# The first feed-forward's gate and up products by the seven-product scheme, in two phases

## The chip, the cores and the metric

The kernel runs on one core of one Trainium2 chip. The metric is the device time of one execution in microseconds (us). Three runs of the kernel before gave 2999.54, 3005.77 and 3012.02 us; the median is 3005.77 us.

## The reference

Two transformer blocks over 1024 tokens of width 1024, in fp32. The change touches the feed-forward of the first block, a gated unit with 2816 = 22 x 128 hidden channels and a convolution over three neighbouring tokens on the gate:

```python
x = x + conv_glu(rmsnorm(x, norm_ffn_g[i]), w_ffn_gate[i], w_ffn_up[i],
                 ffn_conv_w[i], ffn_conv_b[i], w_ffn_down[i])

def conv_glu(h, w_gate, w_up, conv_w, conv_b, w_down):
    S = h.shape[1]
    a = h @ w_gate
    u = h @ w_up
    pad = CONV_WIDTH // 2
    ap = jnp.pad(a, ((0, 0), (pad, pad), (0, 0)))
    c = conv_b
    for j in range(CONV_WIDTH):
        c = c + ap[:, j:j + S] * conv_w[j]
    return (jax.nn.gelu(c, approximate=False) * u) @ w_down
```

The second block's feed-forward, which shares code with it after the change, is `f = square(relu(rms_norm(h) @ w_ff1)); h = h + f @ w_ff2` with 4096 = 32 x 128 hidden channels.

## The kernel before

All activations lie transposed, channels on the 128 partitions and the 1024 tokens along the free axis, so a tile is 128 x 1024. Each fp32 product is made of three matmuls on rounded parts: a weight is split into WH (rounded on ScalarE) and WL (the rest, on GpSimd or VectorE), an activation into H and L, and a product is WH.H + WL.H + WH.L. A matmul has a 128 x 128 weight and 512 token columns. The engines run in the order in which their instructions are written; in the first block's mixing part and the second's two strings of digits set how chains are merged, and elsewhere the code's own order holds.

The first feed-forward is `dense_ffn1` (L1383). For each of the 22 channel tiles m, `gate_up(m)` runs two strips of 48 matmuls (`strip`, L253): 8 input tiles x 3 matmuls x 2 token halves. The gate strip leaves through VectorE (`a`, L1393, times the norm factor R), then the convolution is three VectorE instructions (L1397 to L1399), the gelu is ScalarE's (L531), and GpSimd multiplies by R (L1401). The up strip leaves through a VectorE product with that (L1405), and the result f[m] is split into parts (L699, L700). f stays in SBUF: after each group of FF_PARTS tiles come the down products of that group, added to the residual x (L1326), which stays in SBUF too. Weights come through a ring of four slots (`w_use`), one 512 KB load and one split each (L207, L209).

The second feed-forward already runs in two phases. In `ff1` (L1968) the up products go by the Winograd form of Strassen's algorithm. A unit is two neighbouring channel tiles; the 8 input tiles are 4 pairs. With the activations' blocks x11, x12, x21, x22 and their sums T1 to T4 (`wino_tile`, L610 to L660, made by VectorE in L628, split in L621 and L626) a unit takes seven products of 12 matmuls each (P1 to P7) where the plain form takes eight. Units 0 and 1 come first with P1 and P2 ("lead"), then units 2 and 3 run in the plain form (C11 to C22) while T1 to T4 are being made, then the rest: P6, P5, P7 of a unit, P1 and P2 of the next but one, P4 and P3. The weights' sums S (L428) are GpSimd's, the splits ScalarE's (L452) and VectorE's or, for P1 and P2, GpSimd's (L454); they are prepared up to seven products ahead. Intermediate results are copied out of PSUM by ScalarE (L2005, L2010, L2014) and added by VectorE (L2007, L2016, L2027); relu and the factor R are VectorE's (L2018, L2019, L2028), the square ScalarE's (L2032). P5 and P3 of a unit share one PSUM bank, and two banks (`psd`) serve P5/P3 and P2 in turn. f and the residual go to DRAM (`scr_f`, on SP's queue), and in the second phase, `dense_ff2`, they come back (`fl`, `xr`), f is split again, and the down products run.

## Time and profile before

| | us |
|---|---|
| median of three runs | 3005.77 |
| profiled execution | 3010.28 |
| its span, first to last instruction | 3008.5 |
| TensorE busy (PE) | 2853.0 |
| VectorE busy (DVE) | 1599.3 |
| ScalarE busy (ACT) | 1059.6 |
| GpSimd busy (POOL) | 992.8 |

The profile shows one execution. The 1.8 us between the execution's time and its span lie around the first and the last instruction. Matmuls overlap, so a busy TensorE is judged by the distance from the start of one matmul to the start of the next, not by its busy time. The mean granted clock over the span is 0.98 of full speed.

### The profile page before, as it was taken

How to read it: one execution, taken by the hardware profiler on the slowest of the kernel's cores; microseconds unless marked ns; L12 is line 12 of the kernel's file. 1: busy time of each engine (PE TensorE's matmuls, PEld its weight loads, DVE VectorE, ACT ScalarE, POOL GpSimd, SP SyncE). 2: the span in 40 equal slices, each digit the busy share in tenths (PEclk: the TensorE clock that was granted, in tenths of full speed). 3: DMA queues.
4: the chain of work that ended last, by engine and by line, in shares of the span. 5: the costliest groups of instructions: out<-in, count | busy, mean ns of one | idle time of the engine just before them, and what ended most of it. 6: DMA issues, size and time to landing. Idle time of an engine off the chain costs nothing. (4 is left out here: it accounts for less than half of the span.)

```text
span 3008.5 us, 34910 instructions
## 1 busy us (share of the span) xinstructions
PE 2853.0 (95%) x14216; PEld 2364.8 (79%) x14216; DVE 1599.3 (53%) x1847; ACT 1059.6 (35%) x1480; POOL 992.8 (33%) x630
## 2 busy tenths in 40 slices
PE   8999999989899999999999999878899999999999
PEld 7878878877688888887878787656677778888877
DVE  7377676897732323324336376667685444333343
ACT  4345444554411111111234435454454334211141
POOL 2321115574322322222344244343313432322141
PEclk9999999989999999999999999989899999999999
DMA  3322124231111111111112221133132325422112
GB/s 127 81 53 65 59 74 158 76 120 36 35 42 51 62 36 63 35 50 42 56 56 92 70 71 44 42 112 98 36 112 105 110 108 211 160 78 90 36 56 84
DMA packets 65025, 232.71 MB, mean 77 GB/s; under 512 B 7776, under 2 KB 8544, under 8 KB 64864
## 3 DMA queue, kind: packets, MB, share of 16 engines
q1 hardware_dynamic: 33952, 119.31, 11.0%
q10 hardware_dynamic: 27072, 98.58, 10.3%
q0 software_dynamic: 3840, 12.59, 2.0%
q8 instruction: 112, 1.84, 0.3%
q14 instruction: 49, 0.40, 0.0%
HBM read 170.68 MB, written 46.14 MB: 72 GB/s over the span
## 5 line engine op out<-in xcount | busy, mean ns | idle before, releaser
L209 POOL TENSOR_TENSOR WL<-raw,WH 128x1024 fp32r<-128x1024 f32 x160 | 403.1, 2520 | 918.9 <-ACT WH L207 850.2
L1326 DVE TENSOR_TENSOR xr<-xr,psd 128x512 f32<-128x512 f32 x296 | 202.2, 685 | 389.2 <-PE psd L253 386.7
L253 PE MATMUL ps_f<-xL,WH 128*128 128x512 f32 x832 | 324.7, 390 | 6.3 <-DVE xL L588 6.3
L253 PE MATMUL ps_f<-xH,WH 128*128 128x512 f32 x832 | 325.4, 391 | 3.7 <-DVE xr L1326 3.7
L253 PE MATMUL ps_f<-xH,WL 128*128 128x512 f32 x832 | 323.9, 389 | 0.0
L207 ACT ACTIVATE WH<-raw 128x1024 fp32r<-128x1024 f32 x188 | 197.7, 1053 | 337.0 <-PE psd L253 246.9
L253 PE MATMUL psd<-xH,WH 128*128 128x512 f32 x568 | 233.0, 410 | 2.7 <-DVE cv L1659 1.6
L253 PE MATMUL psd<-xL,WH 128*128 128x512 f32 x568 | 223.6, 394 | 0.0
L253 PE MATMUL psd<-xH,WL 128*128 128x512 f32 x568 | 223.4, 393 | 0.0
L253 PEld LDWEIGHTS ps_f<-xL,WH 128*128 128x128 f32 x832 | 156.5, 188 | 39.7 <-DVE xL L588 7.2
L253 PEld LDWEIGHTS ps_f<-xH,WH 128*128 128x128 f32 x832 | 156.5, 188 | 37.7 <-ACT sq L601 4.1
L253 PEld LDWEIGHTS ps_f<-xH,WL 128*128 128x128 f32 x832 | 156.5, 188 | 33.0 <-issue 0.8
L1401 POOL TENSOR_TENSOR ge<-ge,R 128x1024 f32<-128x1024 f32 x22 | 52.7, 2397 | 387.6 <-ACT ge L531 387.6
L531 ACT ACTIVATE ge<-ge 128x1024 f32<-128x1024 f32 x22 | 23.4, 1062 | 375.7 <-DVE ge L1399 375.7
L280 PE MATMUL psd<-WH,xH 128*128 128x256 f32 x448 | 129.9, 290 | 11.5 <-DVE hgst L977 8.8
L1943 DVE TENSOR_TENSOR_SCAN rem<-rem,ones 128x1024 f32<-128x1024 f32 (+7 forms) x64 | 91.4, 1429 | 81.7 <-POOL rem L1941 81.7
L253 PEld LDWEIGHTS psd<-xH,WH 128*128 128x128 f32 x568 | 108.1, 190 | 26.2 <-issue 4.8
L280 PE MATMUL psd<-WL,xH 128*128 128x256 f32 x448 | 128.0, 286 | 0.7 <-POOL WL L209 0.7
L280 PE MATMUL psd<-WH,xL 128*128 128x256 f32 x448 | 127.8, 285 | 0.0
L253 PEld LDWEIGHTS psd<-xL,WH 128*128 128x128 f32 x568 | 107.7, 190 | 23.7
L253 PEld LDWEIGHTS psd<-xH,WL 128*128 128x128 f32 x568 | 108.0, 190 | 21.7 <-issue 1.7
L469 PE MATMUL psd<-x,WH 128*128 128x512 f32 x352 | 116.6, 398 | 6.8 <-ACT fr L2024 4.6
(853 smaller groups left out, 7095.9 us busy)
## 6 DMA issues: line engine op xcount, KB each, us to landing
raw<-w_in ACTq DMA_DIRECT2D x54, 512.0 KB
scr_f<-fr SPq DMA_DIRECT2D x32, 512.0 KB
fl<-scr_f SPq DMA_DIRECT2D x32, 512.0 KB
raw<-w_ff ACTq DMA_DIRECT2D x32, 512.0 KB
raw<-w_gate ACTq DMA_DIRECT2D x22, 512.0 KB
raw<-w_up ACTq DMA_DIRECT2D x22, 512.0 KB
raw<-w_down ACTq DMA_DIRECT2D x22, 512.0 KB
raw_a<-w_ff SPq DMA_DIRECT2D x18, 512.0 KB
```

The costliest lines, as they stand in the source:

```text
L207: nc.scalar.activation(out=self.WH[:, s], in_=raw, func=AF.Copy)
L209: eng.tensor_tensor(out=self.WL[:, s], in0=raw, in1=self.WH[:, s].bitcast(F32), op=ALU.subtract)
L253: nc.tensor.matmul(ps, a, b[:, hs], start=(i == 0), stop=(i == n - 1))
L280: nc.tensor.matmul(ps, a[:, ts], b, start=(i == 0), stop=(i == 23))
L469: self.nc.tensor.matmul(ps, x[:, js], y, start=(fresh and j == 0 and e == 0), stop=(j == 3 and e == 2), skip_group_check=True)
L531: self.nc.scalar.activation(func=func, **kw)
L1326: self.nc.vector.tensor_tensor(out=self.x[m][:, hs], in0=self.x[m][:, hs], in1=ps, op=ALU.add)
L1401: nc.gpsimd.tensor_tensor(out=ge, in0=ge, in1=self.R, op=ALU.mult)
L1943: nc.vector.tensor_tensor_scan(out=rem[:, 0:w], data0=rem[:, 0:w], data1=self.one_col.to_broadcast([P, w]), initial=1.0, op0=ALU.mult, op1 ...
```

## The change

The first feed-forward gets the second's form. Gate and up strips become units (11 pairs of channel tiles, gate and up in turn, 22 units), and their products go by the seven-product scheme, units 2 and 3 again in the plain form. The residual goes to DRAM on entry (`wino_entry`), f goes to DRAM as it is made, and the down products follow in a phase of their own (`dense_down`, now shared) with the groups (2, 4, 4, 4, 4, 4). The shared code of the up phase is `wino_up`. After a gate tile is done, its convolution, its gelu and its product with R are put on a list, and one of them is issued after each product of 12 matmuls (`todo`); where an up tile needs a factor that is not made yet, the list is run up to it. The product with R moves from GpSimd to VectorE, and so do the WL splits of P1 and P2 in this phase, but for the two lead units. Changed for both feed-forwards: the plain units take C11 and C12 of both units before C21 and C22; the activations' blocks are made in another rhythm (`steps`); and at the start of the phase the weights are prepared at least three products ahead, where it was four. The list of weights in the ring is 44 entries shorter.

```diff
-FF_PARTS = (4, 4, 4, 4, 2, 4)
+FF_PARTS = (2, 4, 4, 4, 4, 4)
...
+    add("w_down", *range(NFF))
...
+def wino_order(n, lead, plain):
+
+    order = [(u, k) for u in range(lead) for k in ("P1", "P2")]
+    order += [(u, k) for ks in (("C11", "C12"), ("C21", "C22")) for u in range(lead, lead + plain) for k in ks]
+    head = len(order)
+    rest = [u for u in range(n) if not lead <= u < lead + plain]
+    order += [(u, "P6") for u in range(2)]
+    for u in rest:
+        order += [(u, k) for k in ("P6", "P5", "P7")[u < 2:]]
+        later = [v for v in rest if v > u and v >= lead]
+        if later and u >= lead - 1:
+            order += [(later[0], "P1"), (later[0], "P2")]
+        order += [(u, "P4"), (u, "P3")]
+    return order, head
...
-        eng = nc.gpsimd if k in ("P1", "P2") else nc.vector
+        eng = nc.gpsimd if k in ("P1", "P2") and (self.wq["n"] < 2 * self.wq["lead"] or self.wq["units"][0][0] == "w_ff1") else nc.vector
...
-            self.wino_ready(i + min(7, max(4, (i - q["head"]) // 2)))
+            self.wino_ready(i + min(7, max(3, (i - q["head"]) // 2)))
...
+    def wino_entry(self, st, m, gname):
+
+        self.wino_tile(st, m, self.x[m], gname, self.scr_f[NFF2 + m])
+        self.x[m] = None
+        if m in (3, 5, 6, 7):
+            self.wino_square(st)
+        if m in (1, 2, 3, 4, 6, 7):
+            self.wino_ready((1, 2, 3, 4, 6, 7).index(m))
...
+                if j == 2 and b == 0:
+                    units = [(mat, 2 * p) for p in range(NFF // 2) for mat in ("w_gate", "w_up")]
+                    self.wino_begin(units, 2, 2)
+                    self.wino_load(3)
...
-                        self.norm_tile(self.st, m, self.x[m], "ffn_g")
+                        self.wino_entry(nst, m, "ffn_g")
...
-            self.merge(self.dense_ffn1(al))
+            self.up1(al)
+            self.merge(self.dense_down("w_down", FF_PARTS, "ple_g"))
...
+    def up1(self, al):
+
+        nc = self.nc
+        g = {}
+
+        todo = self.todo = []
+
+        def factor(u, t):
+            if u % 2 == 0:
+                return self.R
+            while (u - 1, t) not in g:
+                todo.pop(0)()
+            return g[u - 1, t]
+
+        def done(u, t, a):
+            m = u // 2 * 2 + t
+            if u % 2:
+                g.pop((u - 1, t))
+                nc.sync.dma_start(out=self.scr_f[m], in_=a)
+                return
+
+            v = {}
+
+            def conv():
+                ge = v["ge"] = self.U("ge")
+                w = lambda j: self.col("conv_w", j * NFF + m)
+                nc.vector.tensor_scalar(out=ge, in0=a, scalar1=w(1), scalar2=self.col("conv_b", m), op0=ALU.mult, op1=ALU.add)
+                nc.vector.scalar_tensor_tensor(out=ge[:, 0:S - 1], in0=a[:, 1:S], scalar=w(0), in1=ge[:, 0:S - 1], op0=ALU.mult, op1=ALU.add)
+                nc.vector.scalar_tensor_tensor(out=ge[:, 1:S], in0=a[:, 0:S - 1], scalar=w(2), in1=ge[:, 1:S], op0=ALU.mult, op1=ALU.add)
+
+            def gelu():
+                self.act(AF.Gelu, out=v["ge"], in_=v["ge"])
+
+            def times_r():
+                ge = g[u, t] = v.pop("ge")
+                nc.vector.tensor_tensor(out=ge, in0=ge, in1=self.R, op=ALU.mult)
+
+            todo.extend((conv, gelu, times_r))
+
+        self.wino_up(al, factor, lambda out, x, y: nc.vector.tensor_tensor(out=out, in0=x, in1=y, op=ALU.mult), done)
 
...
+    def up2(self, al):
+
+        nc = self.nc
+        self.todo = []
+
+        def done(u, t, y):
+            nc.scalar.activation(out=y, in_=y, func=AF.Square)
+            nc.sync.dma_start(out=self.scr_f[2 * u + t], in_=y)
+
+        self.wino_up(al, lambda u, t: self.R, lambda out, x, y: nc.vector.scalar_tensor_tensor(out=out, in0=x, scalar=0.0, in1=y, op0=ALU.max, op1=ALU.mult), done)
+
+    def wino_up(self, al, factor, mul, done):
+
+        nc = self.nc
+        st, self.st = self.st, None
         norm = self.norm_steps(st)
         plain = []
-
         head = self.wq["head"]
-        steps = lambda i: 3 if i < 2 else 2 if i < 4 or i in (6, 9) or i > head - 3 else 1
+        steps = lambda i: 3 if i < 2 else 2 if i < 4 else 1 if i < 8 else 0 if i < head - 2 else 3 if i < head else 2
 
...
+            if self.todo:
+                self.todo.pop(0)()
             if i > 7 and plain:
-                m, y = plain.pop(0)
-                nc.vector.scalar_tensor_tensor(out=y, in0=y, scalar=0.0, in1=self.R, op0=ALU.max, op1=ALU.mult)
-                done(m, y)
+                u, t, y = plain.pop(0)
+                mul(y, y, factor(u, t))
+                done(u, t, y)
...
             elif k == "P4":
-                nc.vector.scalar_tensor_tensor(out=e["y1"][:, lo], in0=ps, scalar=0.0, in1=R(lo), op0=ALU.max, op1=ALU.mult)
-                nc.vector.scalar_tensor_tensor(out=e["y1"][:, hi], in0=e["y1"][:, hi], scalar=0.0, in1=R(hi), op0=ALU.max, op1=ALU.mult)
-                done(2 * u + 1, e.pop("y1"))
+                y = e.pop("y1")
+                mul(y[:, lo], ps, factor(u, 1)[:, lo])
+                mul(y[:, hi], y[:, hi], factor(u, 1)[:, hi])
+                done(u, 1, y)
...
             else:
-                nc.vector.tensor_tensor(out=e["y0"][:, hi], in0=ps, in1=e.pop("u")[:, lo], op=ALU.add)
-                nc.vector.scalar_tensor_tensor(out=e["y0"], in0=e["y0"], scalar=0.0, in1=self.R, op0=ALU.max, op1=ALU.mult)
-                done(2 * u, e.pop("y0"))
-
-        def done(m, y):
-            nc.scalar.activation(out=y, in_=y, func=AF.Square)
-            nc.sync.dma_start(out=self.scr_f[m], in_=y)
+                y = e.pop("y0")
+                nc.vector.tensor_tensor(out=y[:, hi], in0=ps, in1=e.pop("u")[:, lo], op=ALU.add)
+                mul(y, y, factor(u, 0))
+                done(u, 0, y)
...
             if left == 8:
-                self.halt = len(self.seq)
+                self.halt = self.halts.pop(0)
...
+    def dense_down(self, mat, parts, gname):
+
+        f = self.f
...
+        k0 = blk = 0
+        for j, n in enumerate(parts):
+            last = j == len(parts) - 1
+            ks = range(k0, k0 + n)
+            k0 += n
+            ahead = [] if last else [list(range(k0, k0 + parts[j + 1]))[b * parts[j + 1] // n:(b + 1) * parts[j + 1] // n] for b in range(n)]
+            for b in range(n):
+                s = self.w_use(mat, blk)
+                blk += 1
+                for k in ahead[b] if ahead else []:
+                    if k == len(self.fl):
+                        self.ff_load(k)
+                for i in range(8 // n):
+                    m = 8 // n * b + i
...
+                        self.norm_tile(nst, m, self.x[m], gname)
+                if b and ahead:
+                    for k in ahead[b - 1]:
+                        if k not in f:
+                            self.ff_part(k)
+            for k in ahead[-1] if ahead else []:
+                if k not in f:
+                    self.ff_part(k)
...
-    a["w_up"] = _strips(g["w_ffn_up"][0])
+    a["w_gate"] = _strips(g["w_ffn_gate"][0], True)
+    a["w_up"] = _strips(g["w_ffn_up"][0], True)
```

On VectorE, in the first feed-forward, one channel tile before (`a` is the gate's result, `ge` the factor, `f1L` the low part of f):

```order
L1393 TENSOR_TENSOR a<-ps_f,R 128x512 x2
L1397 TENSOR_SCALAR ge<-a,cols 128x1024
L1398 SCALAR_TENSOR_TENSOR ge<-a,cols,ge 128x1023
L1399 SCALAR_TENSOR_TENSOR ge<-a,cols,ge 128x1023
L1405 TENSOR_TENSOR ge<-ps_f,ge 128x512 x2
L700 TENSOR_TENSOR f1L<-ge,f1H 128x1024
```

And now, from P4 of a gate unit (its `fr<-ps_f,R`) to the convolution of its other tile:

```order
L1430 TENSOR_TENSOR fr<-ps_f,R 128x512
L1430 TENSOR_TENSOR fr<-fr,R 128x512
L1417 TENSOR_SCALAR ge<-fr,cols 128x1024
L1418 SCALAR_TENSOR_TENSOR ge<-fr,cols,ge 128x1023
L1419 SCALAR_TENSOR_TENSOR ge<-fr,cols,ge 128x1023
L443 TENSOR_TENSOR WL<-raw_b,WH 128x512
L2026 TENSOR_TENSOR fr<-psd,u_6776 128x512
L1430 TENSOR_TENSOR fr<-fr,R 128x1024
L443 TENSOR_TENSOR WL<-S_6785,WH 128x512
L1426 TENSOR_TENSOR ge<-ge,R 128x1024
L443 TENSOR_TENSOR WL<-S_6879,WH 128x512
L1417 TENSOR_SCALAR ge<-fr,cols 128x1024
```

The convolution of one tile (L1417 to L1419) now stands ahead of the add that empties the bank of P3 (`fr<-psd,u`, L2026), and the product with R (L1426) stands on VectorE behind a gelu of ScalarE.

On ScalarE, in the second feed-forward before, from one unit's P1 copy (`fr<-ps_f`) to the next unit's P6 copy (`u<-ps_f`):

```order
L2005 COPY fr<-ps_f 128x512
L452 ACTIVATE WH<-raw_a 128x512 x2
L2032 ACTIVATE fr<-fr 128x1024
L452 ACTIVATE WH<-raw_b 128x512
L2032 ACTIVATE fr<-fr 128x1024
L452 ACTIVATE WH<-S_16022 128x512
L2010 COPY u_16152<-ps_f 128x512
```

And in the first feed-forward now, from the same copy of a gate unit to the P6 and P7 copies of the up unit behind it:

```order
L2002 COPY fr<-ps_f 128x512
L441 ACTIVATE WH<-raw_a 128x512 x2
L441 ACTIVATE WH<-raw_b 128x512
L520 ACTIVATE ge<-ge 128x1024
L441 ACTIVATE WH<-S_6785 128x512
L2007 COPY u_6916<-ps_f 128x512
L441 ACTIVATE WH<-S_6879 128x512 x2
L2011 COPY u_6916<-ps_f 128x512
L520 ACTIVATE ge<-ge 128x1024
```

The two squares (L2032) have no counterpart here; a gelu (L520) stands ahead of the P6 copy (L2007), and one behind the P7 copy (L2011).

## Rows read from the trace of the kernel before

**Rows 1.** The page's shares by engine: busy us (share of span) xinstructions.
```profile
PE 2853.0 (95%) x14216; PEld 2364.8 (79%) x14216; DVE 1599.3 (53%) x1847; ACT 1059.6 (35%) x1480; POOL 992.8 (33%) x630
```

**Rows 2.** Three stretches: length; PE, PEld, DVE, ACT, POOL busy; clock; DMA share, GB/s.
```profile
788.10:1524.20 736.10, 725.67 (x3174) 597.73 (x3174) 262.20 (x299) 135.22 (x135) 214.75 (x89) 0.99 0.15 49
...
2285.20:2526.00 240.80, 237.45 (x1034) 193.22 (x1035) 113.83 (x141) 92.38 (x149) 99.06 (x72) 1.00 0.33 121
2537.60:2896.00 358.40, 355.71 (x1560) 291.94 (x1558) 135.07 (x165) 82.18 (x81) 106.64 (x43) 1.00 0.30 103
```

**Rows 3.** TensorE's timeline, first feed-forward: start, duration, line, idle before.
```profile
787.91 0.39 PE L253 MATMUL psd<-oh3L,WH 128*128 128x512 f32 x1
792.00 0.47 PE L253 MATMUL ps_f<-xH,WH 128*128 128x512 f32 x1 [3.71 <-DVE xr L1326]
...
801.49 0.80 PE L253 MATMUL ps_f<-xL,WH 128*128 128x512 f32 x1 [3.99 <-DVE xL L588]
...
1524.17 0.39 PE L253 MATMUL ps_t<-xH,WH 128*128 128x512 f32 x1
```

**Rows 4.** TensorE's timeline, second feed-forward: two product starts in the steady part.
```profile
2512.12 0.39 PE L469 MATMUL ps_f<-x,WH 128*128 128x512 f32 x1
...
2514.84 0.39 PE L469 MATMUL psd<-x,WH 128*128 128x512 f32 x1
```

**Rows 5.** TensorE's matmuls of the second feed-forward's up phase, L469 alone, by count.
```profile
2200.00:2545.00 345.00, 319.10 (x1368) 257.42 (x1368) 0.99 0.32 115
```

**Rows 6.** TensorE's timeline, second feed-forward's up phase: begin, stalls of the start, end.
```profile
2203.47 0.39 PE L469 MATMUL ps_f<-x,WH 128*128 128x512 f32 x1
...
2261.04 0.59 PE L469 MATMUL psd<-x,WH 128*128 128x512 f32 x1 [2.95 <-ACT fr L2024]
...
2285.41 0.49 PE L469 MATMUL ps_f<-xT,WH 128*128 128x512 f32 x1 [0.68 <-ACT u L2014]
...
2537.57 0.39 PE L253 MATMUL psd<-f0H,WH 128*128 128x512 f32 x1
```

**Rows 7.** All engines, end of a unit of the second feed-forward: start, duration.
```profile
2501.45 0.85 DVE L2019 SCALAR_TENSOR_TENSOR fr<-fr,R 128x512 f32<-128x512 f32 x1
...
2503.41 1.30 POOL L428 TENSOR_TENSOR S<-raw_a,S 128x512 f32<-128x512 f32 x1
...
2503.95 1.31 DVE L454 TENSOR_TENSOR WL<-raw_b,WH 128x512 fp32r<-128x512 f32 x1 [1.65 <-ACT WH L452]
2505.19 0.68 DVE L2027 TENSOR_TENSOR fr<-psd,u 128x512 f32<-128x512 f32 x1
...
2507.16 1.06 ACT L2032 ACTIVATE fr<-fr 128x1024 f32<-128x1024 f32 x1 [3.24 <-DVE fr L2028]
...
2508.65 0.56 ACT L2010 COPY u<-ps_f 128x512 f32<-128x512 f32 x1
```

**Rows 8.** TensorE behind that copy.
```profile
2509.26 0.50 PE L469 MATMUL ps_f<-xT,WH 128*128 128x512 f32 x1 [0.30 <-ACT u L2010]
```

**Rows 9.** The gelu chain of the first feed-forward: count, min/median/max ns.
```profile
L1397 DVE TENSOR_SCALAR ge<-a,cols x22: 811/812/814, 813.0 to 1469.7; 128x1024 f32<-128x1024 f32 x22
L1398 DVE SCALAR_TENSOR_TENSOR ge<-a,cols,ge x22: 1283/1284/1287, 813.8 to 1470.5; 128x1023 f32<-128x1023 f32 x22
...
L531 ACT ACTIVATE ge<-ge x22: 1060/1062/1062, 816.4 to 1473.2; 128x1024 f32<-128x1024 f32 x22
```

**Rows 10.** Line L454, all its splits on VectorE of one kind.
```profile
L454 DVE TENSOR_TENSOR WL<-S,WH x56: 679/692/1776, 2258.2 to 2518.4; 128x512 fp32r<-128x512 f32 x56
```

**Rows 11.** Groups in 2295 to 2525 us: count, busy us, mean ns, idle before.
```profile
L428 POOL TENSOR_TENSOR S<-raw_b 128x512 f32<-128x512 f32 x12 | 16.4, 1365 | 0.0
...
L2028 DVE SCALAR_TENSOR_TENSOR fr<-fr,R 128x1024 f32<-128x1024 f32 x12 | 15.5, 1289 | 0.4
...
L2018 DVE SCALAR_TENSOR_TENSOR fr<-ps_f,R 128x512 f32<-128x512 f32 x12 | 8.3, 692 | 21.3 <-PE ps_f L469 21.3
```

**Rows 12.** DMA rate in 2510 to 2600 us, 40 slices of 2.25 us.
```profile
GB/s 297 381 421 401 195 7 233 169 300 229 0 0 0 269 377 364 410 421 419 411 404 417 404 410 410 381 42 0 0 0 0 253 235 302 149 206 27 233 13 220
```

More of the change, by code (lines that the diff above doesn't have):

```diff
@@ L81, in weight_order @@
     add("w_out", *range(8))
-    k = 0
-    parts = []
-    for n in FF_PARTS:
-        parts.append(list(range(k, k + n)))
-        k += n
-    down = {}
-    b = 0
-    for j, n in enumerate(FF_PARTS):
-        nb = n
-        down[j] = list(range(b, b + nb))
-        b += nb
-    emitted = 0
-    for j in range(len(parts)):
-        upto = parts[j][-1] + 1
-        if j + 1 < len(parts):
-            upto += 1
-        while emitted < upto:
-            add("w_gate", emitted)
-            add("w_up", emitted)
-            emitted += 1
-        add("w_down", *down[j])
+    add("w_down", *range(NFF))
     for b in range(2):
@@ L158, in __init__ @@
         self.seq = weight_order()
-        self.halt = next(i for i, e in enumerate(self.seq) if e[0] == "w_ff2")
+        self.halts = [next(i for i, e in enumerate(self.seq) if e[0] == mat) for mat in ("w_down", "w_ff2")]
+        self.after = dict(zip(self.halts, (NFF, NFF2 // 2)))
+        self.halts.append(len(self.seq))
+        self.halt = self.halts.pop(0)
         self.wpos = self.nsplit = self.ndma = 0
@@ L194, in _w_slots @@
                 c = 0
-            if i == self.halt:
-                c = (c + 1) % RING
+            if i in self.after:
+                c = (c + (len(wino_order(self.after[i], 2, 2)[0]) % 8 + 1) // 2) % RING
             out.append(c)
@@ L375, in wino_begin @@
     def wino_begin(self, units, lead, plain):
-        order = [(u, k) for u in range(lead) for k in ("P1", "P2")]
-        order += [(u, k) for u in range(lead, lead + plain) for k in ("C11", "C12", "C21", "C22")]
-        head = len(order)
-        rest = [u for u in range(len(units)) if not lead <= u < lead + plain]
-        order += [(u, "P6") for u in range(2)]
-        for u in rest:
-            order += [(u, k) for k in ("P6", "P5", "P7")[u < 2:]]
-            later = [v for v in rest if v > u and v >= lead]
-            if later and u >= lead - 1:
-                order += [(later[0], "P1"), (later[0], "P2")]
-            order += [(u, "P4"), (u, "P3")]
+        order, head = wino_order(len(units), lead, plain)
         loads = []
@@ L714, in build @@
             self.dram = pool("dram", 1, space=DRAM)
+            self.scr_f = self.dram.tile([NFF2 + KD, P, 1024], F32, name="scr_f")
             self.cst = cst
@@ L859, in block1_mix @@
             self.x = None
-            self.st = dict(H=[], L=[])
             if A_MERGE:
@@ L1829, in dense_out2 @@
         y.clear()
-        nst = dict(X={}, late=[], high=[], low=[], sq=[], nsq=0)
+        nst = self.wino_state()
         for part in range(2):
@@ L1845, in dense_out2 @@
                 if part and b == 0:
-                    early = (1, 2, 3, 4, 6, 7)
                     self.wino_begin([("w_ff1", 2 * i) for i in range(NFF2 // 2)], 2, 2)
@@ L2051, in tail @@
                 self.fast = False
-        self.f = {}
+        X = st["X"]
         self.wino(X, dict(a=al, b=self.ps_d, d=self.ps_d), evac, step, tail)
     def ff_load(self, k):
-        if k == len(self.fl) and k < NFF2:
-            t = self.U("fl")
-            self.nc.sync.dma_start(out=t, in_=self.scr_f[k])
-            self.fl.append(t)
+        t = self.U("fl")
+        self.nc.sync.dma_start(out=t, in_=self.scr_f[k])
+        self.fl.append(t)
     def ff_part(self, k):
```

94 lines of the change are left out of this document (12 added, 82 removed).

## The prediction

> **What bounds the kernel now.** I read the page's shares first, then the three stretches, then TensorE's timeline in them. TensorE is busy 95% of the span and VectorE 53% [rows 1]; in the first feed-forward's 736.1 us VectorE is busy 262 us and ScalarE 135 [rows 2]. So the count of matmuls sets this stage, and what matters beside it is the pace and the pauses. The pace: in the steady part of the second feed-forward two products of 12 matmuls start 2.72 us apart [rows 4], 0.2267 us a matmul. The first feed-forward has 22 x 96 = 2112 gate and up matmuls and 1056 down ones; 3168 x 0.2267 = 718.1 us. It runs from 788.1 (the last matmul before it starts at 787.91) to 1524.17, 736.1 us [rows 3]: 18.0 us are lost, most of them in its start, where two pauses of 3.71 and 3.99 us stand [rows 3] and matmuls run slowly behind them.
>
> The second feed-forward's up phase is the model for what the first becomes. It has 1368 matmuls [rows 5], 310.1 us at that pace, and takes from 2203.47 to 2537.57, 334.1 us [rows 6]: 24.0 lost. I split this. P4 of unit 0 comes after 24 product lengths (4 lead products, 8 plain ones of double length, P6, P6, P5, P7), 65.3 us, so at 2268.8 if nothing waited; it starts at 2285.41 [rows 6], so the start loses 16.6 us. The other 90 products take 252.2 us instead of 244.8, a loss of 7.4, or 0.55 us a unit. That small loss is a queue on ScalarE: the square waits for VectorE's result, starts at 2507.16, and the copy of P6 behind it at 2508.65 [rows 7]; TensorE's P7 waits for the copy until 2509.26 [rows 8].
>
> **The change part by part.**
>
> *Matmuls.* 20 units of 7 products and 2 plain ones of 8 make 156 products, 1872 matmuls, instead of 2112; the down products stay 1056. 240 x 0.2267 = 54.4 us less.
>
> *The start.* The old start's loss of 18.0 goes. The new one has the second feed-forward's entry, blocks, plain units and banks, so I take its 16.6. New is the gelu chain of the plain units: the convolution is 0.81 + 1.28 + 1.28 = 3.4 us of VectorE [rows 9], and the up tile's product forces the gelu and the product with R at once, so VectorE stands until ScalarE has copied two banks and done the gelu (1.06 [rows 9]). Behind the first such place there are 10.9 us of plain products before P6 wants its split, so it is hidden. Behind the second only P6 and P6 (5.4 us) lie before P5, whose split stands behind two bank copies, three block copies, gelu, product with R and the up tile's product: 2 x 0.56 + 3 x 0.6 + 1.06 + 2 x 1.29 + 0.69 = 7.3 us. I add 2 us: 18.6. Bounds: 5 lower if the new rhythm of the blocks helps, 14 higher if both chains (2 x 3.4, 2 x 1.29 for the product with R, and two waits of 2.3 for gelu and copies) land on TensorE whole.
>
> *The steady part.* TensorE needs 14 products, 38.1 us, for a gate and an up unit. VectorE's share for them: 14 splits at 0.69 [rows 10], 6 adds at 0.69, two halves of P4 at 0.69 and 0.85, two full products at 1.29 [rows 7, 11], two convolutions at 3.4 and two products with R at 1.29: 28.7 us, 75%. GpSimd has 8 sums at 1.37 [rows 11], 11 us; ScalarE 14 splits and 6 copies, at 0.6 like the copy in [rows 7], and two gelus, 14 us. Nobody is full; what costs is the order in the queues. The new order puts the convolution ahead of the add that empties P3's bank. From the end of a gate unit's P4: 0.2 until VectorE starts, 0.69 + 0.81 for P4's halves, 3.4, a split and the add at 0.69 each, less the overlaps seen between instructions: the bank is free at 6.1 us, and P5 of the up unit wants it after P3 and P6, at 5.44. That is 0.7 us a pair. Behind it on VectorE stand the splits, but these are seven products ahead. The gelu now stands ahead of the P6 copy: convolution over at 5.0, gelu and a split to 6.7, copy to 7.3; P7 wants it at 8.2, so no wait. The squares with their wait go. So the old loss of 0.55 a unit may go, or stay; 20 x 0.55 = 11 and 10 x 0.7 = 7; I take 15 of the 18. Bounds: 0, since every wait here is at the edge, and 41 (two more waits of 1.3 a pair, below).
>
> *The down phase.* f's splits move here from the up phase; VectorE and ScalarE are busy 135 and 82 us of 358 in the second feed-forward's [rows 2], so they fit. On SP's queue the loads of residual tiles 3 to 7 stand behind the last two stores of f, which wait for VectorE's last products. The first group has only two f tiles, so its strips are half as long (21.8 us for the group) and need a residual tile every 2.72 us. At 410 GB/s [rows 12] one 0.52 MB tile takes 1.3 us; two stores, five residual tiles, two f tiles and three weight blocks are 15.6 us, so it fits with little to spare. The group's end has two splits (f4, f5) where the next group needs them at once: about 1 us. I take 2.5, from 0 to 8. Over the whole stage 60 more transfers of 0.52 MB, 31 MB in some 690 us, are 46 GB/s on top of 49 [rows 2]: hidden.
>
> *The second feed-forward* gets the other rhythm in its start, with 16.6 us to win from; I take 2 us of gain, between 6 gained and 6 lost. That weights further on go to another engine for the split, since the list is 44 entries shorter, I set at 0, plus or minus 2.
>
> Sum: -54.4 - 18.0 + 18.6 + 15 + 2.5 - 2 = -38.3 us. On the profiled execution's 3010.28 that is 2972.0; the median of the runs lies 4.5 us below it, so I predict 2967.5 us.
>
> **A rule weighed.** Around 2503.4 GpSimd runs a sum for 1.30 us, and a split on VectorE that starts at 2503.95 takes 1.31 us [rows 7] where the median is 0.69 and the longest 1.78 [rows 10]. The Trainium skill ("SBUF — State Buffer", section "SBUF: two separate sides") says that VectorE and GpSimd share a port pair as an exclusive lock, and that the one that comes second is blocked for the whole instruction; this trace agrees, with 1.31 us for 0.69. The rule speaks against the change, which moves work to VectorE beside GpSimd's sums; what a sum met at the wrong place would cost is worked out in the first rival, from the rows.
>
> **The rivals.**
>
> *VectorE is held up by GpSimd's sums.* If each gate unit's convolution meets one sum, the bank is free 1.3 us later, 13 us over 10 pairs: 2980.5; if the P7 copy's chain meets one too, 26 us: 2993.5. For it speaks the doubled split [rows 7], against it that GpSimd is busy only 11 of 38 us and loses the splits of P1 and P2 and the product with R. 20%.
>
> *The start is worse.* Both gelu chains land on TensorE: 14 us more, 2981.5. For it: the stall of 2.95 us behind a ScalarE copy [rows 6] is in just this place. 12%.
>
> *The queues come out even.* No square, no late add: steady loss 0, start 14, down phase 1, 4 gained in the second feed-forward: -54.4 - 18.0 + 14 + 1 - 4 = -61.4, less the old loss that may stay, 5: -56, 2949.5. 14%.
>
> *Slower.* GpSimd's four sums of a unit, 5.5 us, run ahead of each P3 add, so that VectorE waits out all of them. For a gate unit 0.7 + 5.5 = 6.2 us; for an up unit, without convolution, the add ends 2.3 us early, so 3.2: 9.4 a pair, 94 us instead of 15. The sum becomes +41, 3046. It decides from 5.3 us a pair on, (38.3 + 15) / 10. Against it: no split on VectorE took over 1.78 us [rows 10], so the two take turns. 3%. In between, with 4 to 5 us a pair, the time would not change: 5%.
>
> **How the numbers follow.** The forecast, 2957 to 2977, has 46%; the others as given. Two in ten left out on both sides make the range 2945 to 2991. About 0.5%, 15 us, is what a measurement of this kernel can tell from no change. Faster than 2990.7: all but half of the last rivals and the worst of the first, 91%; within 0.5%: 6%; slower: 3%.
>
> **What would show it.** TensorE's count falls by 240 matmuls. From the first P1 to P4 of unit 0 it should take 84 us (65.3 + 18.6); then a gate and up pair 38.1 + 1.5 us, with TensorE's longest waits on VectorE's add of P3 (ahead of P5) or on a ScalarE copy; in the down phase one or two waits near its begin. Wrong would be: waits on the splits of weights or on GpSimd's sums in the steady part, a pair of more than 42 us, a lower granted clock outside the start, or a first group that waits for the residual's loads.

## The result and the profile after

The changed kernel takes 2973.56 us (median of four runs, 2970.89 to 2975.06) against 3008.83 for the kernel before: a ratio of 0.9887, 95% interval 0.9862 to 0.9912, so 35 us less. The forecast was 2967.5. Of all the runs reported below one, of the kernel with blocks prepared further ahead, took 3077.3 us at a mean granted clock of 0.873 (0.980 to 0.982 in its others) and is left out. The profiled spans differ by the same 35.2 us (3008.5 and 2973.3), so the sum of the prediction can be held against the trace term by term. The first fence gives the new kernel's busy times by stretch: the first feed-forward's start, from the last output matmul to P4 of unit 0; the rest of its up phase; its down phase; and the second feed-forward's up phase from P4 of unit 0 and down phase (columns as in [rows 2]).

```profile
789.70:874.80 85.10, 73.49 (x293) 58.09 (x292) 68.83 (x88) 42.11 (x70) 12.65 (x5) 0.92 0.21 70
874.80:1238.10 363.30, 360.46 (x1584) 297.02 (x1585) 291.15 (x328) 126.11 (x210) 119.54 (x72) 1.00 0.25 89
1238.10:1493.50 255.40, 246.51 (x1058) 199.55 (x1058) 104.78 (x123) 54.91 (x54) 75.97 (x30) 0.99 0.28 101
2247.70:2502.40 254.70, 248.89 (x1081) 201.84 (x1082) 122.31 (x152) 98.80 (x156) 98.73 (x72) 1.00 0.33 120
2502.40:2854.30 351.90, 350.66 (x1538) 287.73 (x1537) 128.98 (x161) 77.25 (x76) 102.98 (x41) 1.00 0.30 103
```

VectorE, 53% of the span before, is at 81% in the first up phase's first stretch (68.8 of 85.1) and 80% in its long one (291 of 363). Next TensorE's timeline at the borders and the waits of the first feed-forward, to lay beside [rows 3].

```profile
789.51 0.39 PE L252 MATMUL psd<-oh3L,WH 128*128 128x512 f32 x1
794.42 0.77 PE L458 MATMUL ps_f<-x,WH 128*128 128x512 f32 x1 [4.52 <-DVE xr L1327]
...
863.67 0.50 PE L458 MATMUL psd<-xT,WH 128*128 128x512 f32 x1 [2.65 <-ACT WH L441]
866.27 0.80 PE L458 MATMUL psd<-xT,WL 128*128 128x512 f32 x1 [2.10 <-DVE WL L443]
...
874.82 0.50 PE L458 MATMUL ps_f<-xT,WH 128*128 128x512 f32 x1 [0.68 <-ACT u L2011]
...
1238.14 0.39 PE L252 MATMUL psd<-f0H,WH 128*128 128x512 f32 x1
...
1241.46 0.49 PE L252 MATMUL psd<-f0H,WH 128*128 128x512 f32 x1 [1.51 <-DVE fr L2026]
...
1244.78 0.51 PE L252 MATMUL psd<-f0H,WH 128*128 128x512 f32 x1 [1.67 <-DVE xr L1327]
...
1269.34 0.50 PE L252 MATMUL psd<-f5L,WH 128*128 128x512 f32 x1 [2.34 <-DVE f5L L701]
...
1493.45 0.39 PE L252 MATMUL ps_t<-xH,WH 128*128 128x512 f32 x1
```

The stage runs from 789.74 (0.23 behind the last output matmul) to 1493.45: 703.7 us instead of 736.1. The second feed-forward, to lay beside [rows 6, 8]:

```profile
2171.83 0.39 PE L458 MATMUL ps_f<-x,WH 128*128 128x512 f32 x1
...
2177.18 0.50 PE L458 MATMUL ps_f<-x,WH 128*128 128x512 f32 x1 [2.70 <-DVE x L627]
...
2247.71 0.50 PE L458 MATMUL ps_f<-xT,WH 128*128 128x512 f32 x1 [0.68 <-ACT u L2011]
...
2375.82 0.50 PE L458 MATMUL ps_f<-xT,WH 128*128 128x512 f32 x1 [0.30 <-ACT u L2007]
...
2502.39 0.39 PE L252 MATMUL psd<-f0H,WH 128*128 128x512 f32 x1
```

| Term, us | predicted | in the trace | how read |
|---|---|---|---|
| 240 matmuls and the old start gone | -72.4 | -72.4 | by count and [rows 3] |
| new start | +18.6 | +19.8 | 874.82 - 789.74 - 65.3 |
| 132 products after it | +15 | +4.3 | 363.3 - 132 x 2.72 |
| down phase | +2.5 | +15.9 | 255.3 - 239.4 |
| second feed-forward | -2 | -2.8 | up 334.1 to 330.6, down 351.1 to 351.9 |
| the rest | 0 | 0 | what is left of 35.2 |
| sum | -38.3 | -35.2 | |

Two terms were far out and nearly cancelled: the long stretch lost almost nothing, and the down phase six times what it was given. The start had the right size. The three follow with the rows behind them.

*The entry.* These are ScalarE and VectorE ahead of the first P1.

```profile
789.66 1.04 ACT L590 ACTIVATE sq<-xr 128x1024 f32<-128x1024 f32 x1
790.61 0.61 ACT L441 ACTIVATE WH<-raw_a 128x512 fp32r<-128x512 f32 x1
```

```profile
790.78 2.34 POOL L592 TENSOR_TENSOR acc<-acc,sq 128x1024 f32<-128x1024 f32 x1 [3.84 <-ACT sq L590]
```

```profile
791.25 2.42 DVE L443 TENSOR_TENSOR WL<-raw_a,WH 128x512 fp32r<-128x512 f32 x1 [2.75 <-ACT WH L441]
793.60 0.67 DVE L1327 TENSOR_TENSOR xr<-xr,ps_t 128x512 f32<-128x512 f32 x1
794.19 0.68 DVE L1327 TENSOR_TENSOR xr<-xr,psd 128x512 f32<-128x512 f32 x1
```

P1 needs a bank that the last residual tile's adds empty (L1327). On VectorE they stand behind the split of a block that no product wants before 10.9 us later, and that split waits 2.75 us for ScalarE, where a square goes first. The split then takes 2.42 us, beside a GpSimd product, where such a split takes 0.69 alone [rows 10].

*The long stretch.* TensorE at P5 of the up unit, and VectorE's add of the gate unit's P3 (L2026), which the prediction put in its way:

```profile
997.80 0.39 PE L458 MATMUL psd<-xT,WH 128*128 128x512 f32 x1
```

```profile
997.86 0.69 DVE L2026 TENSOR_TENSOR fr<-psd,u 128x512 f32<-128x512 f32 x1
...
1002.91 2.19 DVE L1418 SCALAR_TENSOR_TENSOR ge<-fr,cols,ge 128x1023 f32<-128x1023 f32 x1
```

P5 starts before the add does: it writes the other bank of the pair, the one P2 had left. And a step of the convolution that takes 1.28 us alone [rows 9] takes 2.19 beside a GpSimd sum; still TensorE is busy without a break from 900 to 1230 us.

*The down phase.* VectorE and GpSimd at its begin and at the end of the first group:

```profile
1241.44 2.69 DVE L1430 TENSOR_TENSOR fr<-fr,ge 128x1024 f32<-128x1024 f32 x1
1244.05 1.27 DVE L1327 TENSOR_TENSOR xr<-xr,psd 128x512 f32<-128x512 f32 x2
...
1264.77 1.22 DVE L701 TENSOR_TENSOR f4L<-fl,f4H 128x1024 fp32r<-128x1024 f32 x1
1265.90 3.38 DVE L701 TENSOR_TENSOR f5L<-fl,f5H 128x1024 fp32r<-128x1024 f32 x1
```

```profile
1240.02 3.03 POOL L208 TENSOR_TENSOR WL<-raw,WH 128x1024 fp32r<-128x1024 f32 x1 [38.79 <-PE psd L252]
...
1264.95 3.26 POOL L208 TENSOR_TENSOR WL<-raw,WH 128x1024 fp32r<-128x1024 f32 x1 [3.63 <-ACT WH L206]
```

f's last product and f5's split, 1.23 and 1.22 us alone, take 2.69 and 3.38 beside a GpSimd split of a weight block. Both end about when the GpSimd instruction's end and their own time alone would put it: f5's split at 1269.28, and 1268.21 + 1.22 is 1269.43. The first keeps the residual adds from two banks, the second stands where the next group wants it at once. Behind that pause matmuls start 0.43 us apart instead of 0.23, at the lower of the clock's two levels (1.2 GHz of 2.4; the granted clock is 0.50 from 1270.9 to 1273.9 us):

```profile
1271.37 0.63 PE L252 MATMUL psd<-f4H,WH 128*128 128x512 f32 x1
1271.80 0.63 PE L252 MATMUL psd<-f4H,WL 128*128 128x512 f32 x1
```

### The profile page after: what moved, and what is told of

The parts are those of the page before. It is cut to its first block, busy times and chain, and to the rows that moved or that the text cites. A ratio compares the mean times of both kernels' runs of the same rounds, so it can differ in the third digit from the quotient of the medians.

```text
span 2973.3 us, 35223 instructions
## 1 busy us (share of the span) xinstructions
PE 2805.6 (94%) x13976; PEld 2320.8 (78%) x13976; DVE 1800.7 (61%) x2090; ACT 1150.7 (39%) x1684; POOL 976.3 (33%) x647
## 5 line engine op out<-in xcount | busy, mean ns | idle before, releaser
L208 POOL TENSOR_TENSOR WL<-raw,WH 128x1024 fp32r<-128x1024 f32 x120 | 307.1, 2560 | 992.0 <-ACT WH L206 852.7
L1327 DVE TENSOR_TENSOR xr<-xr,psd 128x512 f32<-128x512 f32 x296 | 202.3, 686 | 393.4 <-PE psd L252 391.0
L206 ACT ACTIVATE WH<-raw 128x1024 fp32r<-128x1024 f32 x144 | 151.9, 1056 | 410.6 <-PE psd L252 276.2
L458 PE MATMUL ps_f<-xT,WH 128*128 128x512 f32 x816 | 269.5, 392 | 7.6 <-ACT u L2007 4.9
L458 PE MATMUL psd<-x,WH 128*128 128x512 f32 x800 | 260.8, 392 | 3.8 <-DVE fr L2004 2.6
L458 PEld LDWEIGHTS ps_f<-xT,WH 128*128 128x128 f32 x816 | 153.3, 188 | 45.5 <-ACT u L2007 9.5
L458 PEld LDWEIGHTS psd<-x,WH 128*128 128x128 f32 x800 | 150.8, 189 | 37.8 <-issue 3.9
L458 PE MATMUL ps_f<-xT,WL 128*128 128x512 f32 x408 | 159.1, 390 | 1.6 <-DVE WL L443 1.5
L458 PE MATMUL psd<-x,WL 128*128 128x512 f32 x400 | 156.2, 391 | 0.0
L443 DVE TENSOR_TENSOR WL<-S,WH 128x512 fp32r<-128x512 f32 x136 | 99.3, 743 | 43.7 <-ACT WH L441 43.5
L1102 DVE TENSOR_REDUCE nm<-ps_s 128x1 f32<-128x1024 f32 x64 | 77.6, 1219 | 49.2 <-PE ps_s L1101 49.1
```

Of the source, the lines that this page charges most:

```text
L206: nc.scalar.activation(out=self.WH[:, s], in_=raw, func=AF.Copy)
L208: eng.tensor_tensor(out=self.WL[:, s], in0=raw, in1=self.WH[:, s].bitcast(F32), op=ALU.subtract)
L443: eng.tensor_tensor(out=WL, in0=src, in1=WH.bitcast(F32), op=ALU.subtract)
L458: self.nc.tensor.matmul(ps, x[:, js], y, start=(fresh and j == 0 and e == 0), stop=(j == 3 and e == 2), skip_group_check=True)
L1102: nc.vector.tensor_reduce(out=nm[:, m:m + 1], in_=sc, axis=AX.X, op=ALU.max, negate=True)
L1327: self.nc.vector.tensor_tensor(out=self.x[m][:, hs], in0=self.x[m][:, hs], in1=ps, op=ALU.add)
```

## The experiments

Each changes the kernel after the change; its medians (three to five runs) stand against 2973.6 us. The kernel before, run beside each in its session, gave medians from 3001.5 to 3008.8 us, so medians of different sessions do not resolve a difference of a few us (the ratios, each to the kernel before of its own session, have intervals of 0.3 to 0.5%). The readings below therefore go by the stretches of the traces.

**The entry.** C11's preparation moves behind the last residual adds. One square moves too: up, from the entry of tile 6 to that of tile 4, and not behind the adds as the expectation says.

```
-        if m in (3, 5, 6, 7):
+        if m in (3, 4, 5, 7):
             self.wino_square(st)
-        if m in (1, 2, 3, 4, 6, 7):
-            self.wino_ready((1, 2, 3, 4, 6, 7).index(m))
+        if m in (1, 2, 3, 4, 7):
+            self.wino_ready(m - 1 if m < 7 else 5)
```

> Preparing the first plain block (C11 of unit 2: a ScalarE copy and a VectorE split) and one square are moved from ahead of the last residual tile's two adds to behind them, in both feed-forwards. Theory: the pause of 4.52 us ahead of the first P1 in the first feed-forward is VectorE's order, the two adds standing behind a split that waits for ScalarE; so the pause falls to 1 us or less, the matmuls at half clock behind it go, P4 of unit 0 comes 4.5 to 6 us sooner after the last output matmul (85.1 us now), the second feed-forward's start (75.9) gains 2, and the whole takes 2966 to 2968 us instead of 2973.6. Rival: the adds are late anyway, or X's last low part is what P1 wants, so that the wait only changes its name: 2972 to 2975.

Measured: 2964.1 us, ratio 0.9873 (0.9852 to 0.9894).

```profile
787.63 0.39 PE L458 MATMUL ps_f<-x,WH 128*128 128x512 f32 x1
...
794.44 0.50 PE L458 MATMUL psd<-x,WH 128*128 128x512 f32 x1 [1.42 <-DVE x L627]
```

P1 follows without a pause. P4 of unit 0 comes 78.9 us after the last output matmul, 6.2 sooner; the second feed-forward's start falls by 3.3, to 72.6. The order of the entry was the cause; the run moves the split and the square together and does not part them.

**The forced gelu.** An up tile is multiplied only when its factor is there.

```
-            if i > 7 and plain:
-                u, t, y = plain.pop(0)
+            now = next((e for e in plain if made(e[0], e[1])), None) if i > 7 else None
+            if now:
+                plain.remove(now)
...
```

> A plain unit's up tile is multiplied only when its factor is made; until then the step takes another tile or none, so no gelu and product with R are forced. Theory: the two waits at P5 of unit 0 (2.65 us on a ScalarE weight copy, 2.10 us on a VectorE weight split) and the slow matmuls behind them come from the forced chain of the second gate tile; they go, the start (85.1 us) gets 5 to 7 us shorter, the total is 2966 to 2969 us. Rival: VectorE has too much to do in the start whatever its order, and the wait moves to P7 or P4 of unit 0: 2972 to 2975.

Measured: 2977.6 us (2971.5 to 2979.0), ratio 0.992 (0.9894 to 0.9945): no gain. The two waits at P5 shrink to one of 0.65, but in their place TensorE waits at P7 and P4:

```profile
866.65 0.50 PE L458 MATMUL ps_f<-xT,WL 128*128 128x512 f32 x1 [2.46 <-DVE WL L443]
...
872.71 0.50 PE L458 MATMUL ps_f<-xT,WH 128*128 128x512 f32 x1 [1.68 <-ACT u L2016]
```

The up phase takes 448.9 us (448.4): the waits moved, as the rival had it. The rival's reason, that VectorE has too much to do in any order, is not shown by this.

**The splits of f.** Each group's splits come after strips 1, 3, 5 and 6 (4 and 6 where the next group has two tiles), and f2 and f3 in the first group instead of the up phase's end; the tiles' loads move with them, to two strips ahead.

```
-            if left in (3, 2):
+            if left == 3 or left == 2 and not self.todo_first:
...
+            cut = {} if last else dict(zip((1, 3, 5, 6) if parts[j + 1] == 4 else (4, 6), range(k0, k0 + parts[j + 1])))
...
+                    if m in cut and cut[m] not in f:
+                        self.ff_part(cut[m])
-                if b and ahead:
-                    for k in ahead[b - 1]:
...
-            for k in ahead[-1] if ahead else []:
...
```

> Down phases of both feed-forwards: the next group's f tiles are split after strips 1, 3, 5 and 6 of a group (4 and 6 for a group of two) instead of after strips 3, 5, 7 and 7; in the first feed-forward f2 and f3 are split in the first group instead of in the up phase's last two steps. Theory: of the 15.9 us lost in the first down phase (255.3 us for 239.4 us of matmuls) the waits of 1.51 and 1.67 us at its begin come from splits ahead of the last unit's adds, and the waits of 2.34 us on f5 and f13 and of some 0.2 to 0.5 us on the other groups' last tiles from splits at the group's end; so it takes 243 to 247 us, the second one (351.9) 349 to 350, and the total is 2961 to 2966 us. Rival: the f tiles' loads (f4 came 8 us after its issue) or the GpSimd splits beside them are what is late: the waits move to other tiles and the total is 2971 to 2976.

Measured: 2961.0 us, ratio 0.9861 (0.9839 to 0.9883). The first down phase falls from 255.3 to 243.5 us, the second from 351.9 to 349.0. TensorE's waits in the first (us in total, times, longest):

```profile
PE psd L252 <- DVE xr L1327: 3.1, 3, 1.5
```

No wait on a split is left. Of the two waits at the begin the first, on the add of P3's bank, is gone with f2 and f3; the second is still 1.51 us, against the theory: f's last product takes 2.72 us beside GpSimd's split in this run too. Two shorter ones are new, 0.46 us behind f4's split and 1.14 behind an add whose residual tile comes late:

```profile
1248.14 1.28 DVE L1327 TENSOR_TENSOR xr<-xr,psd 128x512 f32<-128x512 f32 x2 [1.25 <-DMA xr<-scr_f]
```

**One bank for P5 and P3.** In the first feed-forward's long stretch both products of every unit get the same PSUM bank, P2 the other.

```
+        def same():
+            if not first:
+                return self.ps_d()
+            if self.at < head:
+                return self.ps_d()
+            if not one:
+                one.append(self.ps_d())
+            return one[0]
-        self.wino(X, dict(a=al, b=self.ps_d, d=self.ps_d), evac, step, tail)
+        self.wino(X, dict(a=al, b=self.ps_d, d=same), evac, step, tail)
```

> In the first feed-forward's steady part P5 and P3 of every unit use one and the same PSUM bank, P2 the other. Theory of the prediction: the add that empties P3's bank stands behind the gate unit's convolution and ends about 0.7 us after P5 of the up unit could start, so TensorE waits 0.7 to 0.9 us in each of 9 or 10 pairs, only at the up unit's P5: the up phase gets 6 to 9 us longer and the total is 2979 to 2983 us; this would show that the 15 us forecast were lost only because the two products do not share a bank. Rival: the add is early enough in any case, or its delay is made up: 2972 to 2976 us and no waits on that add.

Measured: 2983.2 us, ratio 0.9942 (0.9923 to 0.996). The place shown above looks like this with one bank:

```profile
1000.19 0.50 PE L458 MATMUL psd<-xT,WH 128*128 128x512 f32 x1 [0.63 <-DVE fr L2028]
```

```profile
999.45 0.68 DVE L2028 TENSOR_TENSOR fr<-psd,u 128x512 f32<-128x512 f32 x1
```

Nine such waits stand between 880 and 1230 us, 9.2 us in all (3.7 at the first, 1.0 at the second, 0.63 or 0.64 at the others), one per pair, only at the up unit's P5; the stretch takes 374.0 us, 10.7 more. The 0.7 us a pair were worked out rightly, for a bank that P5 does not use.

**Sums on VectorE; splits and products on GpSimd.** Two kernels move work between the two engines in opposite directions.

```
-        diff = lambda out, x, y, op=ALU.subtract: (nc.vector if q["nsum"] < q["head"] + 3 else nc.gpsimd).tensor_tensor(out=out, in0=x, in1=y, op=op)
+        diff = lambda out, x, y, op=ALU.subtract: (nc.vector if q["nsum"] < q["head"] + 3 or q["units"][0][0] == "w_gate" else nc.gpsimd).tensor_tensor(out=out, in0=x, in1=y, op=op)
```

> All block sums of the first feed-forward (four a unit, 1.30 to 1.37 us each on GpSimd, 0.69 on VectorE) run on VectorE. VectorE is busy 293 of 365 us in the steady part; 74 sums add some 45 us and the collisions with GpSimd (a convolution step of 1.28 us took 2.19 beside a sum) go. Theory: the weight splits are seven products ahead and VectorE has idle time in each unit, so neither the collisions nor the added work reach TensorE: no new waits in the steady part, total 2971 to 2976 us. Rival (the first one of the prediction, GpSimd's sums hold VectorE up): what waits there are at 887 and 894 us go and the total is 2968 to 2971. Other rival: VectorE, at some 88%, comes late with the adds that empty PSUM: over 2983.

```
-        eng = nc.gpsimd if k in ("P1", "P2") and (self.wq["n"] < 2 * self.wq["lead"] or self.wq["units"][0][0] == "w_ff1") else nc.vector
+        eng = nc.gpsimd if k in ("P1", "P2") else nc.vector
...
-                nc.vector.tensor_tensor(out=ge, in0=ge, in1=self.R, op=ALU.mult)
+                nc.gpsimd.tensor_tensor(out=ge, in0=ge, in1=self.R, op=ALU.mult)
```

> Two pieces go back to GpSimd, as the kernel before had them: the split of P1's and P2's blocks (36 in the first feed-forward) and the gelu's product with R (20). GpSimd gets some 95 us more to do, so more of VectorE's instructions run beside one of its. Theory: collisions cost nothing in the steady part; only the two forced chains of the start get longer by 1.2 us each, so the total is 2973 to 2978 us, with no new waits between 900 and 1230 us. Rival: collisions hold up VectorE's adds and splits so that TensorE waits 1.3 to 2.6 us a pair: 2986 to 3000 us.

Measured: 2973.0 us (0.9877 to 0.9911) with the sums on VectorE, 2990.3 (0.9933 to 0.9966) with more on GpSimd. With the sums on VectorE the up phase is 2.5 us shorter (445.9, 448.4): of the waits at 887 and 894 us, 0.53 and 1.54, one of 0.31 is left, as the rival had it, though the total is the theory's. The stretch from 900 to 1230 us in the kernel after the change, with the sums on VectorE, and with more on GpSimd:

```profile
900.00:1230.00 330.00, 330.00 (x1458) 273.25 (x1457) 261.00 (x297) 112.71 (x190) 112.92 (x68) 1.00 0.27 96
```

```profile
900.00:1230.00 330.00, 329.32 (x1453) 272.39 (x1452) 272.35 (x365) 113.11 (x191) 0.00 (x0) 1.00 0.26 94
```

```profile
900.00:1230.00 330.00, 324.08 (x1421) 265.77 (x1420) 268.59 (x239) 110.09 (x186) 203.02 (x119) 1.00 0.26 91
```

Read VectorE's column (the third) and GpSimd's (the fifth). 68 sums more raise VectorE's busy time by only 11 us, though they are 68 x 0.685 = 47 us of work: the other 35 were its own instructions held up beside GpSimd's 113 us. And 58 instructions fewer do not lower it: it rises by 7.6. The splits of the sums' blocks show it one by one, in the same three kernels:

```profile
L443 DVE TENSOR_TENSOR WL<-S,WH 128x512 fp32r<-128x512 f32 x70 | 50.1, 728 | 8.4 <-ACT WH L441 8.4
```

```profile
L443 DVE TENSOR_TENSOR WL<-S,WH 128x512 fp32r<-128x512 f32 x69 | 46.5, 684 | 3.6 <-ACT WH L441 3.6
```

```profile
L443 DVE TENSOR_TENSOR WL<-S,WH 128x512 fp32r<-128x512 f32 x70 | 88.9, 1288 | 8.0 <-ACT WH L441 7.6
```

My theory fell for the second kernel: the held-up convolution makes the gelu late on ScalarE, the copy of P6 stands behind the gelu, and TensorE waits for the copy at P7, 0.75 us in each of eight pairs.

```profile
1004.64 1.06 ACT L520 ACTIVATE ge<-ge 128x1024 f32<-128x1024 f32 x1 [8.85 <-DVE ge L1419]
...
1006.12 0.57 ACT L2007 COPY u<-ps_f 128x512 f32<-128x512 f32 x1
```

```profile
1006.74 0.50 PE L458 MATMUL ps_f<-xT,WH 128*128 128x512 f32 x1 [0.75 <-ACT u L2007]
```

The start is 2.7 us longer too, the whole up phase 14.3. So the change's moves to VectorE were worth some 14 us by the traces here, 17 by the medians: they took from GpSimd what holds VectorE up.

**Entry and splits together.**

> The edits of the first and the third experiment together. Theory: the two act at different places (the first product of each up phase; each group's end and the begin of the down phase), each removes pauses of TensorE with the slow matmuls behind them, and so they add up: 9.5 and 12.5 less, 2950 to 2954 us. Rival: the earlier start only brings a later stage's loads or VectorE's backlog nearer, and less than half of the smaller gain is kept: 2957 to 2961 us.

Measured: 2948.7 us, ratio 0.9816 (0.9796 to 0.9837). They add up: up and down phases take 442.8, 243.2, 326.9 and 349.0 us, 24.2 less in all.

**Blocks prepared further ahead**, with both edits and the unforced gelu.

```
-            self.wino_ready(i + min(7, max(3, (i - q["head"]) // 2)))
+            self.wino_ready(i + min(7, max(3 if i < 7 else 5, (i - q["head"]) // 2)))
```

> As the run with both edits; besides, the up tile is multiplied only when its factor is made (as in the second experiment), and from the last plain products on the blocks are prepared five products ahead instead of three. In the second experiment the waits moved from P5 of unit 0 to the following products because VectorE is 91% busy from 790 to 900 us. Theory: VectorE's idle 3.8 us at 829 to 833, where it waits for a ScalarE copy of a block that is not asked for yet, is now used, so the backlog behind the plain units is 3 to 4 us smaller: 3 to 6 us less than with both edits alone, 2945 to 2950 us. Rival: VectorE has too much to do until 900 us whatever its order: as with both edits alone, within 1.5 us.

Measured: 2950.5 us (2950.9 if the run left out is counted), 0.9818 (0.9799 to 0.9838). The waits of P5 and P7 turn into one at P4 of unit 0, and one of 2.67 us stands at 914:

```profile
862.83 0.80 PE L458 MATMUL ps_f<-xT,WH 128*128 128x512 f32 x1 [5.90 <-ACT u L2018]
```

The up phase takes 443.7 us, 442.8 with the two edits alone: no gain, as the rival had it. But the run does not decide between the two, since VectorE's idle 3.8 us, which the theory wanted to use, still stand:

```profile
823.50 0.69 DVE L443 TENSOR_TENSOR WL<-raw_b,WH 128x512 fp32r<-128x512 f32 x1 [3.80 <-ACT WH L441]
```

The 91% of the expectation is 90.9 us of the 110 from 790 to 900 us in the kernel after the change, so 83%.

**The old rhythm in the second feed-forward.**

```
+    cut = (("C11", "C12", "C21", "C22"),) if n == NFF2 // 2 else (("C11", "C12"), ("C21", "C22"))
...
+            self.wino_ready(i + min(7, max(4 if q["units"][0][0] == "w_ff1" else 3, (i - q["head"]) // 2)))
...
+        steps = lambda i: 3 if i < 2 else 2 if i < 4 or second and (i in (6, 9) or i > head - 3) else 1 if i < 8 or second else 0 if i < head - 2 else 3 if i < head else 2
```

> The second feed-forward alone gets back what the change altered for both: its blocks in the old rhythm, its plain products unit by unit (C11, C12, C21, C22 of one unit, then of the other), its weight blocks prepared four products ahead. Theory: these made its start 6.0 us shorter (75.9 us to P4 of unit 0, 81.9 before) and its steady part 2.5 us longer (254.7 us, 252.2 before); so both go back and the total is 2976 to 2978 us. Rival: the shorter start comes from what stands ahead of it (where the earlier stages leave the queues and buffers), so the start stays at 76 and the total at 2972 to 2975 us.

Measured: 2975.5 us, 0.9901 (0.9885 to 0.9917). The total lies between the two; the trace decides: start 81.9 us (75.9), the rest of the up phase 252.5 (254.7). Both are close to the figures of the kernel before (81.9 and 252.2), so the three things that went back made the difference together, and not what stands ahead of the phase. The run does not part the blocks' rhythm from the plain products' order and the preparation four products ahead.

```profile
2169.43:2251.36 81.93, 71.91 (x294) 56.53 (x292) 61.03 (x81) 44.51 (x72) 11.04 (x5) 0.96 0.22 77
```

**The square one product later.**

```
-            nc.scalar.activation(out=y, in_=y, func=AF.Square)
-            nc.sync.dma_start(out=self.scr_f[2 * u + t], in_=y)
+            def square():
+                nc.scalar.activation(out=y, in_=y, func=AF.Square)
+                nc.sync.dma_start(out=self.scr_f[2 * u + t], in_=y)
+
+            self.todo.extend((lambda: None, square))
...
```

> The second feed-forward's square (ScalarE) and its store are issued one product later, so that ScalarE does the copy of P6 before the square that waits for VectorE. Theory, that of the prediction's steady term: ScalarE's order is what costs 0.46 us a unit at P7 (11 such waits in the trace, two more of 1.79 and 0.64), so they go and the second feed-forward's steady part (254.7 us) gets 5 to 7 us shorter: 2966 to 2969 us. Rival: the copy is late because the bank's last product ends late or weight copies stand ahead of it, and the waits stay: 2972 to 2975 us.

Measured: 2969.2 us, 0.9879 (0.9863 to 0.9895).

```profile
2248.45:2495.89 247.44, 246.76 (x1080) 203.84 (x1081) 127.62 (x150) 100.87 (x157) 103.44 (x72) 0.99 0.36 128
```

The second up phase from P4 of unit 0 falls from 254.7 to 247.4 us, where 90 products take 244.8: the queue on ScalarE was the loss. Part is given back in the start, where P4 of unit 0 now waits 4.49 us for ScalarE's copy of P7.

**All four, and the plain units' squares at once again.**

> The edits of the first and third experiment, the block sums of both feed-forwards on VectorE, and the later square, together. Theory: each acts where the trace had its wait, so with 2948.7 us for the first two, 5 to 7 us less from the square and 2 to 3 from the sums, the total is 2938 to 2942 us. Rival: with the sums VectorE is late for the square or for the start's splits, and the total is 2944 to 2950 us.

```
+            if u in (2, 3):
+                square()
+            else:
+                self.todo.extend((lambda: None, square))
```

> As the run with all four edits, but the squares of the second feed-forward's plain units are issued at once again; only those of the other units come a product later. Theory: the pause that the later square brought at P7 of unit 0 (3.48 us here, 4.49 us with that edit alone, on a ScalarE copy, with slow matmuls behind it) comes from the plain units' squares, which now stand between that copy and the products of the start; it goes back to the 0.5 us that the kernel after the change has there, so 3 to 5 us less than with all four: 2935 to 2938 us. Rival: the copy stands behind X's copies and weight copies in any order, and the time stays at 2939 to 2941 us.

Measured: 2939.8 us, ratio 0.9783 (0.9763 to 0.9802), and 2937.1, 0.9774 (0.9757 to 0.9791). In the last one the pause (which stands at P4, not at P7 as the expectation says) is back to 0.68 us, the start 72.6 and the rest of the phase 245.9 us:

```profile
2219.83:2465.74 245.91, 245.24 (x1081) 202.76 (x1082) 137.48 (x199) 100.24 (x156) 32.00 (x24) 1.00 0.35 124
```

Its trace's second up phase is 3.7 us shorter than with all four edits; the medians, 2.7 apart, have overlapping intervals. It beats both kernels, the one after the change by 36 us.

## Why the prediction was right or wrong

*Matmuls.* Right: the count sets the stage, at 2.72 us a product.

*The total.* It came within 6 us of the forecast, but by luck: the steady part was 10.7 us better than its term and the down phase 13.4 worse.

*The start.* Right in size, 18.6 and 19.8, and half right in cause. The analog of the second feed-forward gave 16.6, but in the first the pause ahead of P1 is 4.52 us, on the adds of the residual, and no term has it: without it, in the first run, the start loses 78.9 - 65.3 = 13.6. The stop of 2.95 us at a ScalarE copy [rows 6] is down to 0.4 in both new starts; the ninth run, with the old order in the second, has it again. The chain behind the second plain place was named and priced at 2 us; at P5 it costs 2.65 + 2.10. That it "forces the gelu" is not all that costs: unforced, the waits move and the time stays. Whether VectorE's work or an order of it that was not tried is the bound there stays open.

*The steady part.* Wrong: 15 predicted, 4.3 measured, and of those nothing between 900 and 1230 us. The step that failed is "the add that empties P3's bank ... P5 of the up unit wants it": its times hold (0.63 us in the one-bank kernel), its bank does not. I took the two products of consecutive units to share a bank without following which of the two is free first. The other half, the 0.55 us a unit that "may go, or stay", went with the squares; the tenth run shows that the square's place in ScalarE's queue is nearly all of that loss. That the gelu makes no wait ("copy to 7.3; P7 wants it at 8.2") held, by a margin that the sixth run's held-up convolution used up.

*The down phase.* Wrong, 2.5 for 15.9. The step is the sentence on the group's end, "about 1 us". It left out that every group ends so, five times, that a split there takes 3.38 us and not 1.22 when GpSimd has a weight block (twice, 2.34 us each), that some 1.5 us of slow matmuls stand behind each of these two pauses, and that VectorE brings a backlog from the last unit (1.51 + 1.67). By the starts of the matmuls the begin costs 4.0 us, the ends on f5 and f13 4.6 each and the other three 0.8 each. The third run took back 11.8 us of it. The residual's loads were no limit, as said; in the third run one is, for 1.1 us.

*The second feed-forward.* Right in size, -2 and -2.8, and in that the gain lies in the start. But -2 was a net of two effects of which the prediction has one: the altered start won 6.0 and lost 2.5 behind it, as the ninth run shows for its three parts together.

*The first rival.* VectorE held up by GpSimd's sums came about as a mechanism, at a small price in this kernel: without the sums the up phase is 2.5 us shorter (fifth run). The splits run seven products ahead, and the adds that empty PSUM are not held up themselves (last section). The Trainium skill ("SBUF — State Buffer", section "SBUF: two separate sides") has the pair of engines share a lock; the traces agree, by the starts and ends of the instructions. The convolution step at 1002.91 began with 1.11 us of a GpSimd sum to run (1002.22 to 1004.02) and took 0.91 longer than alone; f5's split had 2.31 us of GpSimd's split ahead of it and took 2.16 longer. The Trainium skill's "Perfetto Trace Analysis" (section "Optimizing Scalar/DVE Operations") warns that work moved between these two might not help; here moving it back to GpSimd cost 14 us by the traces.

## What to carry to other kernels

A loss per unit taken from a model stage has to be tied to its instruction first: here it was a square that the new stage does not have. Whether a late add costs anything depends on which buffer the waiting product gets, so follow the allocation, not the product's name. And work that is needed at once at a group's end belongs a strip earlier: that and the order of the entry were worth 25 us.

## What the hardware showed

A split, a product or a convolution step of VectorE, all operands in SBUF, that starts while a GpSimd instruction runs takes longer by what that one still has to run, less 0.1 to 0.2 us (38 of 39 cases in the first feed-forward that begin at least 0.4 us into the other): 2.19 us instead of 1.28 for a convolution step (1.11 us to run), 3.38 instead of 1.22 for a split (2.31 to run). The profile counts this as VectorE's busy time. GpSimd's sums take longer too, 1.57 to 1.74 us on average instead of 1.30 [rows 7]. VectorE's adds with one operand in PSUM are not held up: those of P2 (L2004) took 0.68 to 0.69 us in all 30 cases of the sixth run in which a GpSimd instruction ran throughout. With GpSimd left idle VectorE does 47 us more work in 11 us more busy time.
